# A new order of the 35 DMA transfers of a batched matmul-and-subtract kernel

## Chip, cores, metric

The kernel runs on one core of a Trainium2 chip. The metric is device time per execution in microseconds (us). A run is called slow when it is over 1.5% above the fastest of its kernel; ratios use the other runs, called fast.

## The reference

```python
batch, m, k, n = 16, 512, 1024, 768
def reference(x, weight, sub_value):          # all float32
    return (np.matmul(x, weight) - sub_value).astype(np.float32)
```

The 8192 rows are worked as 64 "m tiles" of 128. In memory terms: x is 33.6 MB, sub_value and the result 25.2 MB each, the weight 3.1 MB, 87.0 MB in all.

## The kernel before

All transfers are issued by one engine (SyncE) in the order of a table. Each entry is a kind (x, weight chunk, sub_value, output), a first tile and a number of tiles. SyncE waits for what an entry needs, issues it, and goes to the next; so a transfer whose wait isn't over also holds back those after it.

```python
TRANSFERS = [
    ('x', 0, 1), ('w', 0, 1), ('x', 1, 1), ('w', 1, 1), ('x', 2, 2), ('w', 2, 1),
    ('w', 3, 1), ('x', 4, 4), ('s', 0, 5), ('x', 8, 8), ('s', 5, 3), ('s', 8, 8),
    ...
    ('o', 48, 10), ('o', 58, 4), ('o', 62, 1), ('o', 63, 1),
]
...
            need, by = {                      # what must be done before this entry is issued
                "w": (set(), "o"),
                "x": ({t for t in old if t >= 0}, "cast"),     # the x ring holds 16 tiles
                "s": ({t for t in old if t >= 0}, "o"),        # sub_value/output ring: 32 tiles
                "o": (span, "finish"),
            }[kind]
```

ScalarE casts each x tile to fp16. The tile is then transposed, 40 tiles on TensorE (ScalarE evicts them) and 24 on VectorE. TensorE multiplies in four chunks of the weight, and VectorE subtracts sub_value in place ("finish"), after which the tile may be stored. PSUM has three output buffers, so tile 3 cannot be multiplied before tile 0 is finished. Casts, transposes and finishes run in fixed orders on their engines.

```python
NX, NSO = 16, 32
N16, NXT, NPT, NPO = 4, 5, 2, 3               # NPO: outputs in PSUM
...
    idle(9)                                   # filler matmuls that keep the TensorE clock up
    cast(2)
    cast(3)
    transpose_tile(2)
    transpose_tile(3)
    for c in range(n_c):
        matmuls(2, c)
    finish(2)
    for mi in range(HEAD + 1, HEAD + TA):     # tile 4
        cast(mi)
        transpose_tile(mi)
```

## Time and profile before

| | before |
|---|---|
| time, median of 3 runs, at the time of the prediction | 211.04 us (210.6 to 211.05) |
| span of the profiled execution | 208.5 us |
| TensorE busy | 195.9 us (94%) |
| VectorE busy | 147.4 us (71%) |
| share of the 16 DMA engines taken by the kernel's queue | 98.0% |
| bytes moved | 87.03 MB |

In the page's slice rows, each of the 40 digits is a fortieth of the span: busy tenths for an engine, tenths of full clock for PEclk, mean busy tenths of the 16 DMA engines for DMA. The thing to notice is that two resources, TensorE and DMA, look full at once, while the chain of work that ended last names only one.

### The profile page before, as it was taken

How to read it: one execution, taken by the hardware profiler on the slowest of the kernel's cores; microseconds unless marked ns; L12 is line 12 of the kernel's file. 1: busy time of each engine (PE TensorE's matmuls, PEld its weight loads, DVE VectorE, ACT ScalarE, POOL GpSimd, SP SyncE). 2: the span in 40 equal slices, each digit the busy share in tenths (PEclk: the TensorE clock that was granted, in tenths of full speed). 3: DMA queues.
4: the chain of work that ended last, by engine and by line, in shares of the span. 5: the costliest groups of instructions: out<-in, count | busy, mean ns of one | idle time of the engine just before them, and what ended most of it. 6: DMA issues, size and time to landing. Idle time of an engine off the chain costs nothing.

```text
span 208.5 us, 2449 instructions
## 1 busy us (share of the span) xinstructions
PE 195.9 (94%) x1216; PEld 75.7 (36%) x704; DVE 147.4 (71%) x266; ACT 103.1 (49%) x105; POOL 0.7 (0%) x6
## 2 busy tenths in 40 slices
PE   7959879999999999999999999999999999999970
PEld 2413434443343434343434333343434343344420
DVE  0231043369999999998899969999999999423330
ACT  2640556976446371916463275537291821467400
POOL 1000000000000000000000000000000000000000
PEclk9996999999999999999999999999999999999998
DMA  6999999999999999999999999999999999999994
GB/s 198 424 437 425 458 437 383 457 405 438 433 445 429 439 421 422 442 429 420 408 463 431 417 430 442 445 386 430 434 426 447 424 431 434 443 446 395 460 390 199
DMA packets 4906, 87.17 MB, mean 418 GB/s; under 512 B 544, under 2 KB 544, under 8 KB 1568
## 3 DMA queue, kind: packets, MB, share of 16 engines
q1 hardware_dynamic: 4896, 87.03, 98.0%
q8 instruction: 7, 0.11, 0.2%
q14 instruction: 3, 0.02, 0.0%
HBM read 61.87 MB, written 25.17 MB: 417 GB/s over the span
## 4 chain that ended last, share of the span: by engine, by line
PE 88%; DMA 5%; ACT 1%; SPq 1%; DVE 1%; issue 0%
PE po_b L180 79%; PE pt_b L317 8%; DMA so_ring<-in_weight_dram 5%; ACT xt_b L324 1%; PE po_b L405 1%; SPq L280 1%; DVE w_sb L247 0%; DVE so_ring L388 0%; ACT x_b L299 0%; SPq L244 0%; SPq L517 0%; SPq L134 0%
## 5 line engine op out<-in xcount | busy, mean ns | idle before, releaser
L180 PE MATMUL po_b<-w_sb,xt_b 128*128 128x384 f16 x640 | 113.3, 329 | 3.5 <-DVE w_sb L247 2.6
L344 DVE STREAM_TRANSPOSE xtp_b<-x16p_b 32x256 f32<-32x256 f32 x192 | 83.6, 435 | 8.2 <-ACT x16p_b L299 5.2
L388 DVE TENSOR_TENSOR so_ring<-po_b,so_ring 128x768 f32<-128x768 f32 x64 | 60.0, 956 | 34.7 <-PE po_b L180 21.6
L324 ACT COPY xt_b<-pt_b 128x1024 f16<-128x1024 f16 x40 | 40.4, 1012 | 81.4 <-PE pt_b L317 81.0
L180 PE MATMUL po_b<-w_sb,xtp_b 128*128 128x384 f16 x384 | 73.6, 326 | 0.0
L368 PEld LDWEIGHTS <-xt_b 128*128 128x128 f16 x320 | 31.7, 99 | 63.2 <-issue 60.3
L299 ACT CAST x_b<-x_ring 128x1024 f16<-128x1024 f32 x40 | 41.5, 1045 | 8.8 <-DMA x_ring<-in_x_dram 8.7
L317 PE MATMUL pt_b<-ident,x_b 128*128 128x128 f32 x160 | 41.1, 273 | 1.3 <-ACT x_b L299 1.3
L317 PEld LDWEIGHTS pt_b<-ident,x_b 128*128 128x128 f32 x160 | 22.0, 141 | 34.8 <-issue 31.6
L299 ACT CAST x16p_b<-x_ring 128x1024 f16<-128x1024 f32 x24 | 25.1, 1046 | 3.9 <-DMA x_ring<-in_x_dram 3.8
L368 PEld LDWEIGHTS <-xtp_b 128*128 128x128 f16 x192 | 18.8, 98 | 21.9 <-issue 20.1
L247 DVE CAST w_sb<-so_ring 128x768 f16<-128x768 f32 x8 | 4.1, 557 | 11.8 <-DMA so_ring<-in_weight_dram 11.8
L405 PE MATMUL po_b<-idle_x,idle_w 128*128 128x512 f16 x31 | 9.3, 454 | 1.5 <-DVE idle_x L399 1.5
L405 PEld LDWEIGHTS po_b<-idle_x,idle_w 128*128 128x128 f16 x31 | 3.5, 114 | 5.9 <-issue 2.7
L299 ACT ACT_TABLE_LOAD x1 | 1.3, 1283 | 0.9 <-SPq L134 0.9
L398 DVE MEMSET idle_w<- 128x64 uint32 x1 | 0.1, 112 | 1.0 <-SPq L134 1.0
L418 PE MATMUL po_b<-idle_x,idle_w 128*128 128x512 f16 x1 | 0.4, 379 | 0.0
L169 POOL TENSOR_SCALAR_AFFINE_SELECT ident<-ident 128x128 f32<-128x128 f32 x1 | 0.3, 292 | 0.1
L399 DVE MEMSET idle_x<- 128x256 uint32 x1 | 0.3, 272 | 0.0
L168 POOL MEMSET ident<- 128x128 f32 x1 | 0.2, 206 | 0.5 <-SPq L134 0.5
L418 PEld LDWEIGHTS po_b<-idle_x,idle_w 128*128 128x128 f16 x1 | 0.1, 98 | 0.1
L506 POOL MEMSET const-bfloat16-1.0<- 128x1 bf16 x1 | 0.1, 102 | 0.0
(3 smaller groups left out, 0.3 us busy)
## 6 DMA issues: line engine op xcount, KB each, us to landing
so_ring<-in_sub_value_dram SPq DMA_DIRECT2D x2, 3840.0 KB, 20.1
x_ring<-in_x_dram SPq DMA_DIRECT2D x2, 3584.0 KB, 18.7
x_ring<-in_x_dram SPq DMA_DIRECT2D x2, 3072.0 KB, 23.0
out_dram<-so_ring SPq DMA_DIRECT2D x2, 3072.0 KB, 30.4
out_dram<-so_ring SPq DMA_DIRECT2D x1, 6144.0 KB, 32.9
x_ring<-in_x_dram SPq DMA_DIRECT2D x1, 5120.0 KB, 17.4
so_ring<-in_sub_value_dram SPq DMA_DIRECT2D x2, 2304.0 KB, 16.7
x_ring<-in_x_dram SPq DMA_DIRECT2D x1, 4608.0 KB, 19.7
```

Of the source, the lines that this page charges most:

```text
L169: pool.add(lambda: nc.gpsimd.affine_select(out=ident, in_=ident, compare_op=mybir.AluOpType.not_equal, fill=1.0, base=0, pattern=[[-1, P]] ...
L180: return nc.tensor.add_instruction(mybir.InstMatmult(name=nc.get_next_instruction_name(), engine=full.engine, ins=list(full.ins), outs=lis ...
L247: lambda at=at, r=r, st=st: nc.vector.tensor_copy(out=w_sb[:, at, r], in_=st[:, r]),
L280: sp.add(lambda here=here, there=there: nc.sync.dma_start(out=here, in_=there), waits, (sem, 16))
L299: act.add(lambda: nc.scalar.copy(out=to, in_=x_in), waits, count("cast"))
L317: pe.add(lambda: nc.tensor.transpose(words, from_, ident), waits, count("turn") if last else None)
L324: act.add(lambda: nc.scalar.copy(out=xt_b[:, d], in_=pt_b[:, b]), waits, count("evac"))
L344: dve.add(lambda: nc.vector.transpose(xt[b * Q : (b + 1) * Q, :, a * Q : (a + 1) * Q], x16[a * Q : (a + 1) * Q, :, b * Q : (b + 1) * Q],), ...
L368: pe.add(lambda weights=weights: nc.tensor.ldweights(weights, tile_position=(0, 0)), [w for w in waits if w[0] in ready])
L388: dve.add(lambda: nc.vector.tensor_tensor(out=o, in0=po[:, :, :NS], in1=o, op=mybir.AluOpType.subtract), [landed["s", mi], (counter["mul"] ...
L405: lambda: nc.tensor.matmul(po_b[:, NPO - 1, 0], idle_w, idle_x, start=True, stop=True),
L418: pe.add(lambda: nc.tensor.matmul(po_b[:, NPO - 1, 0], idle_w, idle_x, start=True, stop=True), [(counter["ident"], 2)])
```

## The change

The intent is that each load of the steady part be asked for well before the queue has worked off what stands in front of it (at least two thirds of a transfer). The weights come ahead of x tiles 2 and 3, some transfers are cut differently, and the last store holds two m tiles instead of one.

```diff
 TRANSFERS = [
-    ('x', 0, 1), ('w', 0, 1), ('x', 1, 1), ('w', 1, 1), ('x', 2, 2), ('w', 2, 1),
-    ('w', 3, 1), ('x', 4, 4), ('s', 0, 5), ('x', 8, 8), ('s', 5, 3), ('s', 8, 8),
-    ('x', 16, 3), ('s', 16, 5), ('x', 19, 6), ('x', 25, 7), ('s', 21, 11), ('o', 0, 8),
-    ('x', 32, 7), ('o', 8, 8), ('s', 32, 6), ('x', 39, 9), ('s', 38, 10), ('x', 48, 10),
-    ('o', 16, 9), ('o', 25, 7), ('s', 48, 6), ('s', 54, 10), ('x', 58, 6), ('o', 32, 16),
-    ('o', 48, 10), ('o', 58, 4), ('o', 62, 1), ('o', 63, 1),
+    ('x', 0, 1), ('w', 0, 1), ('x', 1, 1), ('w', 1, 1), ('w', 2, 1), ('w', 3, 1),
+    ('x', 2, 2), ('x', 4, 4), ('s', 0, 4), ('x', 8, 2), ('s', 4, 4), ('x', 10, 6),
+    ('s', 8, 8), ('x', 16, 3), ('x', 19, 6), ('s', 16, 9), ('x', 25, 7), ('o', 0, 8),
+    ('s', 25, 7), ('x', 32, 6), ('o', 8, 8), ('s', 32, 5), ('x', 38, 10), ('s', 37, 11),
+    ('x', 48, 7), ('x', 55, 3), ('o', 16, 6), ('o', 22, 10), ('s', 48, 6), ('x', 58, 6),
+    ('s', 54, 10), ('o', 32, 16), ('o', 48, 10), ('o', 58, 4), ('o', 62, 2),
 ]
```

## The prediction

> **What bounds the kernel now.** I read the page's DMA and engine rows first, then engine and DMA sums over two long stretches, then the transfers' issue-to-landing times, then the start and the end in the timeline. One core, span 208.5 us in the profiled execution, 211.04 us as the median of the timed runs; I carry the difference of 2.5 us along as constant.
>
> The page, DMA part and chain:
>
> ```profile
> PEclk9996999999999999999999999999999999999998
> DMA  6999999999999999999999999999999999999994
> q1 hardware_dynamic: 4896, 87.03, 98.0%
> ...
> PE 88%; DMA 5%; ACT 1%; SPq 1%; DVE 1%; issue 0%
> ```
>
> The chain of work that ended last says "PE 88%", but it follows releases, and a transfer that stands in the DMA queue behind others is not a release. The DMA row says the other half: every slice between the first and the last is at 9 tenths or more. The sums over 3 to 103 and 103 to 203 us (columns: stretch, its length, busy us of PE, PEld, DVE, ACT, POOL with instructions, granted clock, DMA share, GB/s):
>
> ```profile
> 3.00:103.00 100.00, 95.13 (x579) 37.36 (x345) 67.22 (x122) 52.93 (x55) 0.00 (x0) 0.98 1.01 428
> 103.00:203.00 100.00, 99.21 (x636) 37.80 (x354) 79.63 (x143) 48.87 (x50) 0.00 (x0) 1.00 1.00 431
> ```
>
> The 16 DMA engines are at share 1.00 for 200 us running and move 429 GB/s. So there is no hole in the DMA stream to be filled. TensorE is also nearly always busy. The two run neck and neck, and the DMA bytes (87.03 MB) are the same before and after.
>
> How far ahead are the loads asked for already? From the DMA view cut to the moment of an issue (KB, then us to landing), the four tightest of the later part, each from its own stretch:
>
> ```profile
> x_ring<-in_x_dram SPq DMA_DIRECT2D x1, 5120.0 KB, 17.4
> ```
>
> ```profile
> so_ring<-in_sub_value_dram SPq DMA_DIRECT2D x1, 2304.0 KB, 11.9
> ```
>
> ```profile
> so_ring<-in_sub_value_dram SPq DMA_DIRECT2D x1, 3840.0 KB, 14.6
> ```
>
> ```profile
> out_dram<-so_ring SPq DMA_DIRECT2D x1, 384.0 KB, 4.0
> ```
>
> At 429 GB/s their own bytes take 12.2, 5.5, 9.2 and 0.9 us, so 5.2, 6.4, 5.4 and 3.1 us were something else. The very first transfer, with nothing before it, takes 4.1 us for 0.52 MB (1.2 us), hence 2.9 us of pure overhead. So the tightest loads stood 2.3 to 3.5 us in the queue behind others, and only the last store (0.2 us) met a queue that was about to run dry. "Ahead enough" is already true of every load.
>
> The start, from the timeline of TensorE and VectorE (start, us, engine, line, operation, count, idle before it and releaser):
>
> ```profile
> 14.45 1.03 DVE L247 CAST w_sb<-so_ring 128x768 f16<-128x768 f32 x2 [3.35 <-DMA so_ring<-in_weight_dram]
> 16.32 1.03 DVE L247 CAST w_sb<-so_ring 128x768 f16<-128x768 f32 x2 [0.85 <-DMA so_ring<-in_weight_dram]
> 25.89 2.69 DVE L388 TENSOR_TENSOR so_ring<-po_b,so_ring 128x768 f32<-128x768 f32 x3 [8.54 <-DMA so_ring<-in_sub_value_dram]
> ```
>
> ```profile
> 15.53 4.44 PE L180 MATMUL po_b<-w_sb,xt_b 128*128 128x384 f16 x16 [2.27 <-DVE w_sb L247]
> ...
> 23.45 2.77 PE L180 MATMUL po_b<-w_sb,xt_b 128*128 128x384 f16 x16 [0.67 <-ACT xt_b L324]
> 26.06 0.60 PE L317 MATMUL pt_b<-ident,x_b 128*128 128x128 f32 x4
> 26.90 0.81 PE L180 MATMUL po_b<-w_sb,xt_b 128*128 128x384 f16 x4 [0.24 <-DVE so_ring L388]
> ```
>
> TensorE waits 2.27 us for the third chunk of the weight and then runs 16 matmuls in 4.44 us instead of 2.6 because its clock fell to half. Tile 3 starts at 26.90, released by the first subtraction, which itself waited for the first sub_value load (PSUM holds three outputs, so tile 3 needs tile 0's). One more wait of 1.00 us (a cast) follows inside tile 3; after 28.7 TensorE never waits again and reaches the last matmul at 202.25.
>
> **What the Trainium skill says.** "DMA: Bandwidth & Descriptors", Specifications, gives a fabric ceiling of 435 GB/s and an HBM limit of about 358 GB/s per core. The trace sits at 429, so it agrees with the first and contradicts the second; 99% of the ceiling is reached. The same page, Anatomy of one DMA, says that DMA engines do not wait on semaphores, the issuing sequencer does, and puts about 2 us of fixed cost on a transfer (fitted on another issue path); here the first transfer shows 2.9 us. "TensorE: Matmul & The Clock Gate", Part 1, says that an idle window of about 3.4 us halves the clock. This trace halves it after 2.27 us of idleness, for one such window (the 6 in PEclk), which costs about 1.7 us of TensorE work.
>
> **The change, part by part.** No compute instruction is added or removed; 34 transfers become 35, same bytes.
>
> (a) One more transfer: 128 more packets. A 3 KB row takes 121 ns and a 48 KB row 1815 ns in the trace's packet records, so 8 ns each beyond the bytes: 128 x 8 / 16 engines = 0.06 us.
>
> (b) Weights ahead of x tiles 2 and 3. Those x tiles are 1.05 MB, 2.4 us. The third chunk lands at 14.4 - 2.4 = 12.0, its casts end at 13.0, and TensorE is done with chunk 2 at 13.3: the 2.27 us wait and the slow clock go. The fourth chunk is cast by 14.9, so chunks 3 and 4 end at about 16.2 instead of 19.97. Nine filler matmuls (1.9) follow, then transposes (0.6, x tiles 2 and 3 having landed at 16.3 and been cast at 17.3) and an eviction (1.0): tile 2 starts at about 19.9 instead of 23.45, **3.5 us earlier**, and ends at 22.6 (2.77 us), tile 4's transposes at 23.2.
>
> (c) But tile 3 waits for sub_value. Ahead of it are now 7.34 MB + a 1.57 MB load of four tiles: it lands 3.7 us (1.57 MB) after x 4 to 7, which land at 21.2 as before, so 24.9 instead of 25.85. With a subtraction of 0.96 us, tile 3 starts at **25.9 instead of 26.9**. The 3.5 us shrink to 1.0; a gap of some 2.7 us stands before tile 3, and may halve the clock there (1.7 us). The 1.00 us wait for a cast in tile 3 goes, as ScalarE gets through its queue earlier. Lead of TensorE at tile 4: 2.0 to 2.3 us, or about 0.4 with the halved clock.
>
> (d) Splitting x 8 to 15 in 2 + 6 moves x 10 to 15 from 36.3 to about 38.3-39 (14.68 MB in all). The cast of tile 12, in ScalarE's order ahead of tile 8's eviction, waits for it; tile 8's eviction ends at 40.4-41.1, just about when a TensorE that leads by 2 us wants it (41.0). VectorE's first transposes start at 42.5 instead of 43.45, and its subtraction of tile 8 then ends at 49.8 where tile 11 wants it at 49.7. So VectorE allows a lead of about 1.3 to 2 us, no more.
>
> (e) The steady part. Summing bytes at 429 GB/s and taking the releases from the casts and subtractions of the trace less 1 to 2 us, x 38 to 47 is issued at about 99 with a queue until 106, x 48 to 54 at 119 with one until 128, sub_value 48 to 53 at 146 with one until 155, 54 to 63 at 155 with one until 168. All longer than before, and worth nothing: the queue wasn't empty before. The DMA stream stays at share 1.00.
>
> (f) The last store. Before: issued at 203.25, 4.0 us. After: two tiles, 2.9 + 1.8 = 4.7 us from its issue, which comes at 203.25 less the lead. With a lead of 0.4 to 2.0 it lands on TensorE's account at 207.5 to 206.0; on the DMA queue's account at about 207.0 (207.25 less the 0.2 us of near-empty queue). The later counts: **207.0 to 207.5 against 207.25**.
>
> The sum: -0.25 to +0.25 us, plus 0.06. I put it at 210.9 us.
>
> **Rivals.** (1) *TensorE is the bound*, as the chain says: then the lead of 2 us shows in full, 209.0 us. Against it: DMA share 1.00 and bytes unchanged; 87.03 MB at 429 GB/s are 202.9 us, plus 2.2 us before the first packet and about 2 us from last byte to end, which is all of the span. (2) *The start gets worse*: gap before tile 3 with a halved clock, plus stalls on tile 12's cast and on VectorE, leave TensorE 1 us late; the two-tile store adds 0.7: 212.5 to 213 us. For it: gap and late x 10 to 15 are real. Against it: I count a lead even with the halved clock. (3) *The new mix moves faster*: slices of the GB/s row vary from 383 to 463, but that is packets counted where they start; both 100 us stretches give 428 and 431, so at most some tenths of a us.
>
> **Range and chances.** Centre 210.9; low end if the queue's tail packs better and runs fall as the fastest of before (210.6) do, 209.7; high end from rival 2, 212.8. A gain over 2% needs 206.8, below what the bytes take: 0.02. A loss over 2% needs 215.3, a TensorE late by 4 us and more: 0.04.
>
> **What would show it.** Right: DMA share 1.00 throughout; tile 2's matmuls at about 19.9; the first subtraction at about 24.9 and tile 3 at 25.9 after a gap of 2 to 3 us; ScalarE idle until 38 to 39 for x; the last subtraction ending 0.4 to 2 us before 203.2 while the span hardly moves. Wrong: a DMA slice of steady time below 9 tenths, a last subtraction later than before, or a span that follows TensorE's lead.

## The result

The changed kernel takes 210.49 us (median of 6 runs, 210.23 to 210.66), the kernel before 210.63 us in the same comparison (6 runs, 210.17 to 211.05). The ratio is 0.9991 with a 95% interval of 0.9973 to 1.0008: the same. A ratio is the mean time of one kernel's fast runs over that of the other's of the same rounds, so it is not quite the ratio of the medians quoted.

The programs of TensorE, VectorE, ScalarE and GpSimd are the same in the two kernels but for which landing they wait for; only the DMA issues differ. The page of the changed kernel, the same rows as shown of before:

```profile
PEclk9999969999999999999999999999999999999996
DMA  5999999999999999999999899999999999999984
q1 hardware_dynamic: 5040, 87.03, 98.0%
...
PE 84%; DMA 10%; SPq 2%; DVE 1%; issue 0%; DVEq 0%
```

The DMA row has the same shape and the same 98.0%. The slow slice of the clock has moved from the fourth to the sixth slice (26 to 31 us). The sums over the two long stretches (busy us and counts by engine, clock, DMA share, GB/s):

```profile
3.00:103.00 100.00, 95.97 (x583) 37.89 (x347) 68.26 (x125) 53.34 (x55) 0.00 (x0) 0.98 1.01 428
103.00:203.00 100.00, 98.56 (x632) 37.61 (x352) 78.69 (x140) 48.05 (x50) 0.00 (x0) 1.00 1.00 430
```

They show 428 and 430 GB/s, where before had 428 and 431: the stream was full and stayed full. The start, from the timeline of VectorE and TensorE:

```profile
11.79 1.03 DVE L247 CAST w_sb<-so_ring 128x768 f16<-128x768 f32 x2 [0.85 <-DMA so_ring<-in_weight_dram]
...
24.82 2.69 DVE L388 TENSOR_TENSOR so_ring<-po_b,so_ring 128x768 f32<-128x768 f32 x3 [10.11 <-DMA so_ring<-in_sub_value_dram]
```

```profile
19.71 2.78 PE L180 MATMUL po_b<-w_sb,xt_b 128*128 128x384 f16 x16 [0.67 <-ACT xt_b L324]
22.32 0.60 PE L317 MATMUL pt_b<-ident,x_b 128*128 128x128 f32 x4
...
25.83 0.81 PE L180 MATMUL po_b<-w_sb,xt_b 128*128 128x384 f16 x4 [2.91 <-DVE so_ring L388]
...
27.56 1.48 PE L180 MATMUL po_b<-w_sb,xt_b 128*128 128x384 f16 x4
```

The third weight chunk arrives 2.7 us earlier and tile 2 starts at 19.71 instead of 23.45. Then TensorE stands 2.91 us until the first subtraction, which waits for its load of sub_value; its clock halves (four matmuls take 1.48 us instead of 0.81), and of the 3.7 us lead 0.6 us are left. The last subtraction, before and after, and the store after it (KB, us to landing):

```profile
202.25 0.96 DVE L388 TENSOR_TENSOR so_ring<-po_b,so_ring 128x768 f32<-128x768 f32 x1 [1.64 <-PE po_b L180]
```

```profile
201.59 0.96 DVE L388 TENSOR_TENSOR so_ring<-po_b,so_ring 128x768 f32<-128x768 f32 x1 [1.64 <-PE po_b L180]
out_dram<-so_ring SPq DMA_DIRECT2D x1, 768.0 KB, 4.6
```

The store goes out at 202.6 and lands at 207.2. In the kernel before it was issued at 203.2 and landed at 207.25.

### The profile page after: what moved, and what is told of

Its sections match the earlier page's. It is cut to its first block, busy times and chain, and to the rows that moved or that the text cites. A ratio compares the mean times of both kernels' runs of the same rounds, so it can differ in the third digit from the quotient of the medians.

```text
span 208.5 us, 2450 instructions
## 1 busy us (share of the span) xinstructions
PE 196.1 (94%) x1216; PEld 76.1 (36%) x704; DVE 147.3 (71%) x266; ACT 102.7 (49%) x105; POOL 0.7 (0%) x6
## 4 chain that ended last, share of the span: by engine, by line
PE 84%; DMA 10%; SPq 2%; DVE 1%; issue 0%; DVEq 0%
PE po_b L180 77%; DMA so_ring<-in_sub_value_dram 10%; PE pt_b L317 7%; DVE so_ring L388 1%; SPq L244 1%; SPq L280 1%; SPq L517 0%; DVEq L56 0%; SPq L134 0%
## 5 line engine op out<-in xcount | busy, mean ns | idle before, releaser
L388 DVE TENSOR_TENSOR so_ring<-po_b,so_ring 128x768 f32<-128x768 f32 x64 | 60.0, 955 | 37.1 <-PE po_b L180 25.9
L405 PE MATMUL po_b<-idle_x,idle_w 128*128 128x512 f16 x31 | 9.9, 477 | 1.5 <-DVE idle_x L399 1.5
L418 PE MATMUL po_b<-idle_x,idle_w 128*128 128x512 f16 x1 | 0.4, 379 | 0.0
```

Of the source, the lines that this page charges most:

```text
L388: dve.add(lambda: nc.vector.tensor_tensor(out=o, in0=po[:, :, :NS], in1=o, op=mybir.AluOpType.subtract), [landed["s", mi], (counter["mul"] ...
L405: lambda: nc.tensor.matmul(po_b[:, NPO - 1, 0], idle_w, idle_x, start=True, stop=True),
L418: pe.add(lambda: nc.tensor.matmul(po_b[:, NPO - 1, 0], idle_w, idle_x, start=True, stop=True), [(counter["ident"], 2)])
```

## Experiments

Theory A: the DMA stream bounds the time, and TensorE's lead counts for nothing as long as the last store is issued before the queue is empty. Rival B: TensorE is the bound, as the chain says, and its lead was eaten by the halved clock and by the longer last store. "Lead" means how much earlier a matmul starts than the same matmul in the one profile of the kernel before. Two profiles of one order already differ by up to 0.3 us in this count, as e2 shows below, so a lead is good to about that.

### Four edits of the ends: e1 to e4

e1 is the changed kernel with two single stores at the end:

```diff
-    ... ('o', 62, 2),
+    ... ('o', 62, 1), ('o', 63, 1),
```

> The changed order, with the last two m tiles stored by two transfers again. Theory A (the DMA stream is the bound; TensorE's lead counts only in the last microsecond): the dip of the DMA share at 202 to 204 us goes, the last landing moves from 207.2 to 206.8-207.0, the time is 0.2 to 0.5 us below the changed kernel, so about 0.3 us below the kernel before (ratio 0.998). Rival B (TensorE is the bound and its lead of 0.66 us is what counts): the whole 0.66 us shows, and a lone one-tile store saves another 0.6: about 1.2 us below the kernel before (0.994).

e2 is the kernel before with the opposite edit, its last two stores made one.

> The kernel before with only its last two stores made one. Both theories: TensorE ends at 202.2 as before, the store is issued at 203.2 and takes 4.6-4.7 us instead of 4.0, so 0.5 to 0.7 us slower than the kernel before (ratio 1.002 to 1.003). A rival C, that one larger store is cheaper at the end because it has one completion less: 0.1 to 0.3 us faster.

e3 is the changed kernel with fillers in the gap before tile 3 (into a transposition buffer whose content has been evicted). e4 is e3 with e1's stores.

```diff
     for mi in range(HEAD + 1, HEAD + TA):
         cast(mi)
         transpose_tile(mi)
+    for _ in range(13):
+        pe.add(
+            lambda: nc.tensor.matmul(pt_b[:, 1].bitcast(F32), idle_w, idle_x, start=True, stop=True),
+            [(counter["evac"], evac_at[3])],
+        )
```

> The changed kernel with 13 filler matmuls in the gap before tile 3, so that the clock is not halved. Both theories: no half-speed window at 26 to 31 us, TensorE's lead over the kernel before grows from 0.66 to about 2 us, the last subtraction starts near 200.2. Theory A: the span falls by at most 0.3 us against the changed kernel (last landing 206.9), because the DMA queue ends when it ends. Rival B: the span falls by the whole 1.3 us, to 207.2 (ratio to the kernel before 0.993).

> Fillers in the gap and two single stores at the end: the best that the parts promise. Theory A: no more than e1 or e3 alone, last landing 206.7 to 206.9, ratio to the kernel before 0.997 to 0.999. Rival B: lead 2 us and a short last store, 2.5 us less, ratio 0.988.

All four are correct, and ran on one chip with the same runs of the kernel before (median 210.94, 11 runs between 210.32 and 212.31, a noisier set than elsewhere):

| run | median us | ratio to before (95%) | lead at tile 4 | lead at tile 62 |
|---|---|---|---|---|
| changed kernel (earlier comparison) | 210.49 | 0.9991 (0.9973 to 1.0008) | 0.61 | 0.65 |
| e1 split last store | 210.62 | 0.9975 (0.9943 to 1.0007) | 2.13 | 0.80 |
| e2 merged last store, old order | 210.56 | 0.9982 (0.9945 to 1.0019) | 0.29 | -0.20 |
| e3 fillers in the gap | 210.72 | 0.9983 (0.995 to 1.0016) | 2.35 | 0.73 |
| e4 both | 210.45 | 0.997 (0.9938 to 1.0002) | 2.20 | 0.66 |

None differs from the kernel before beyond its interval, and the ratios that Rival B gave for e3 (0.993) and e4 (0.988) lie outside the intervals measured. e2 issues the same transfers as the kernel before up to its last store and has the same compute, so its 0.29 and -0.20 are what chance alone does to a lead. The clock row and a timeline line of e3:

```profile
PEclk9999999999999999999999999999999999999997
```

```profile
22.68 2.97 PE L446 MATMUL pt_b<-idle_x,idle_w 128*128 128x512 f16 x13
25.76 0.81 PE L180 MATMUL po_b<-w_sb,xt_b 128*128 128x384 f16 x4
```

The fillers do what they should: no halved clock, and a lead of 2.35 us at tile 4. The time does not follow, which Rival B needed. The second thing in the table wasn't expected in this form: all leads of the new order end at 0.65 to 0.80 us. In e3 the lead is 2.35 at tile 6, 1.36 at tile 12 and 0.71 at tile 40. The first cut comes where the prediction put it, at tiles 8 to 12, where TensorE waits for VectorE's subtractions (matmuls released by it at 50 and 53 us). The second comes at tiles 38 to 40, again released by VectorE; VectorE's transposes of tile 40 wait there 2.23 us for a cast, and the cast 2.71 us for the load of x 38 to 47, which lands at 119.5. So the DMA stream itself takes the lead back.

By chance e1's profiled run shows the same without fillers:

```profile
25.98 0.81 PE L180 MATMUL po_b<-w_sb,xt_b 128*128 128x384 f16 x4 [2.92 <-DVE so_ring L388]
```

Its gap before tile 3 was 2.92 us long, yet its clock did not halve. The clock records say what the chance was. While the kernel runs, the granted clock changes only at steps of 3.41 us, whose position differs from run to run. Here is the step before the halved one and the halved one, in the kernel before and in the changed one, and the two steps over which e1's gap lies (PE's busy time comes third; the clock is the third number from the end):

```profile
12.22:15.63 3.41, 1.14 (x8) 0.29 (x3) 1.03 (x2) 1.99 (x2) 0.00 (x0) 1.00 1.06 438
15.63:19.05 3.42, 3.42 (x12) 0.87 (x6) 1.03 (x2) 0.00 (x0) 0.00 (x0) 0.50 1.00 426
```

```profile
23.71:27.12 3.41, 1.29 (x9) 0.47 (x5) 2.30 (x3) 2.15 (x3) 0.00 (x0) 1.00 1.04 428
27.12:30.53 3.41, 3.41 (x13) 1.32 (x8) 0.39 (x1) 0.00 (x0) 0.00 (x0) 0.50 1.06 449
```

```profile
20.87:24.28 3.41, 2.20 (x15) 0.96 (x9) 0.00 (x0) 2.22 (x3) 0.00 (x0) 1.00 0.97 407
24.28:27.70 3.42, 1.72 (x12) 0.71 (x7) 2.69 (x3) 1.73 (x2) 0.00 (x0) 1.00 1.03 426
```

TensorE was busy for 33% and 38% of the steps that a halved one follows; e1's gap was split, and left 64% and 50%. Counted over all 14 traces, the 35 full-clock steps that a halved one follows are busy for at most 0.44 of their length, the 752 that a full one follows for at least 0.40. (Busy times of matmuls are modelled, so the border is rough.)

The clock also gives a test without new runs. Of e1's six runs, three have a mean clock of 0.992, the profiled one among them, and took 210.35, 210.67 and 210.75 us; the three with a halved step (0.977 to 0.982) took 210.47, 210.58 and 210.79. TensorE's gain does not show in the time.

e2 lost nothing, against an expected 0.5 to 0.7 us. Its end and that of the changed kernel, by microsecond (the last two columns are DMA share and GB/s):

```profile
202.00:203.00 1.00, 0.41 (x3) 0.00 (x0) 0.56 (x1) 0.00 (x0) 0.00 (x0) 1.00 0.92 393
203.00:204.00 1.00, 0.00 (x0) 0.00 (x0) 0.40 (x1) 0.00 (x0) 0.00 (x0) 1.00 0.55 233
204.00:205.00 1.00, 0.00 (x0) 0.00 (x0) 0.00 (x0) 0.00 (x0) 0.00 (x0) 1.00 0.89 375
```

```profile
202.00:203.00 1.00, 0.00 (x0) 0.00 (x0) 0.55 (x1) 0.00 (x0) 0.00 (x0) 1.00 0.92 393
203.00:204.00 1.00, 0.00 (x0) 0.00 (x0) 0.00 (x0) 0.00 (x0) 0.00 (x0) 1.00 0.87 369
204.00:205.00 1.00, 0.00 (x0) 0.00 (x0) 0.00 (x0) 0.00 (x0) 0.00 (x0) 0.81 0.93 387
```

The queue does run thin in e2 (0.55 at 203 to 204 us), but its store, issued at 203.4, lands 4.0 us later at 207.4, only 0.15 us after the one-tile store of before. So this dip costs a few tenths at most, and these are not seen in the times.

### Relieving one bound, then the other: e5 to e7

Three kernels with wrong results, all from the changed kernel. e5 leaves out half of the matmuls, e6 stores only the first half of the tiles of each store, e7 does both.

```diff
     def matmuls(mi, c):                       # e5, e7
+        if c in (1, 2):
+            return
...
             if kind == "o":                   # e6, e7
-                here, there = there, here
+                keep = max(1, n // 2)
+                here, there = there[:, :keep], here[:, :keep]
```

> The changed kernel with the matmuls of chunks 2 and 3 of the four left out (a wrong result on purpose): TensorE has about 94 us less to do, all transfers as before. Theory A: the DMA share stays at 1.00 and the time falls by at most 0.6 us, 209.7 to 210.5. Rival B (TensorE bounds): tens of microseconds less, 120 to 160 us.

> The changed kernel with each store halved to its first half of the tiles (a wrong result on purpose): 12.6 MB less, 29 us of the DMA stream. Theory A with TensorE close behind: TensorE's own chain (start at 25.8, 175.8 us of work to 201.6, subtraction, store) takes over as the bound, so the time falls by little, 1 us at most (the last store is one tile and not two): 209.5 to 210.3. A pure DMA bound with TensorE far behind would give 181 us.

> Both reliefs at once (wrong on purpose). Theory A (two bounds neck and neck): only now does the time fall much, to about 178 to 188 us, the DMA stream of 74.4 MB at 429 GB/s (173.5 us) plus start and end and what VectorE's and ScalarE's chains hold back. If neither alone nor both moved it, a third bound (VectorE, 147 us busy, or ScalarE) would be the one.

| run | TensorE busy us | MB | median us | ratio to before (95%) |
|---|---|---|---|---|
| e5 half of the matmuls | 131.0 | 87.0 | 210.33 | 0.9995 (0.998 to 1.0009) |
| e6 half of the stores | 195.7 | 74.5 | 207.37 | 0.9859 (0.9842 to 0.9875) |
| e7 both | 126.9 | 74.5 | 193.47 | 0.9194 (0.918 to 0.9207) |

e5, its engine row and DMA row, and the last store (KB, us to landing), issued at 192.1:

```profile
PE 131.0 (63%) x704; PEld 51.8 (25%) x448; DVE 147.2 (71%) x266; ACT 102.2 (49%) x105; POOL 0.7 (0%) x6
...
DMA  6999999999999999999999999999999999999993
```

```profile
out_dram<-so_ring SPq DMA_DIRECT2D x1, 768.0 KB, 15.2
```

This is the clearest result. A third of TensorE's busy time is gone (65 us, not the 94 that I had expected), the last store is ready more than 10 us earlier, and it lands at 207.3 all the same, after 15.2 us mostly in the queue. The DMA stream sets the end, and the chain view, which had said "PE 88%", had not seen it. That view is no steady witness either: in e1, which computes the same, it says

```profile
DMA 40%; PE 36%; DVE 10%; ACT 6%; SPq 2%; issue 2%; ACTq 0%
```

e6 shows how close the second bound is. Its DMA row and last store:

```profile
DMA  5999999999999999999799999999999995009031
```

```profile
out_dram<-so_ring SPq DMA_DIRECT2D x1, 384.0 KB, 2.3
```

Here the queue is empty at the end, TensorE's chain ends as in the changed kernel (last subtraction at 201.6), and the time is 3.0 us lower. I had expected 1 us at most, because I had taken 2.9 us of overhead for a transfer that meets an empty queue. The measured store takes 2.3 us for 0.39 MB; less 0.9 us for its bytes at 429 GB/s, that is 1.4. e6's two longer stores before it, and all three such stores of e7, give 1.4 to 1.5 as well. So TensorE's chain would end 1.4 us before the DMA stream in the changed kernel, not with it: the two profiled spans, both with a halved clock at the start, differ by 2.3 us (208.5 and 206.2), less the 0.9 us by which e6's one-tile store is shorter. The median of e6 is lower by more because three of its four runs kept the full clock (0.998 to 1.0) and took 207.25 to 207.47 us, against 207.97 for the profiled one (0.986). Here, where TensorE is the bound, the halved step costs 0.5 to 0.7 us; in e1 it cost nothing.

e7 lands above its expected 178 to 188. The chain of e7:

```profile
DVE 65%; DMA 17%; PE 7%; issue 5%; SPq 3%; ACT 2%; ACTq 0%
```

With both relieved, the chain names VectorE's transposes and subtractions. But the chain was wrong above, and from 62 to 172 us two resources are full again, VectorE with 106.98 us of 110 and DMA with a share of 0.99:

```profile
62.00:172.00 110.00, 71.70 (x406) 27.47 (x242) 106.98 (x203) 56.35 (x58) 0.00 (x0) 0.94 0.99 416
```

No run relieves VectorE, so which of them sets e7's time is not shown. What is shown: relieving DMA alone is worth 1.4%, relieving TensorE and DMA together 8%.

### The start alone: e8

The kernel before with only the weights moved ahead of x tiles 2 and 3.

```diff
-    ('x', 0, 1), ('w', 0, 1), ('x', 1, 1), ('w', 1, 1), ('x', 2, 2), ('w', 2, 1),
-    ('w', 3, 1), ('x', 4, 4), ...
+    ('x', 0, 1), ('w', 0, 1), ('x', 1, 1), ('w', 1, 1), ('w', 2, 1), ('w', 3, 1),
+    ('x', 2, 2), ('x', 4, 4), ...
```

> The kernel before with only the weights moved ahead of x tiles 2 and 3, all other transfers as before. Both theories: tile 2's matmuls start near 19.8, the first subtraction at 25.9 as before, tile 3 at 26.9 after a gap of 3.7 us with a halved clock after it; the wait of 1.0 us for a cast in tile 3 goes. TensorE's lead between -0.7 and +1.0 us. Theory A: time within 0.5 us of the kernel before unless TensorE comes out late; rival B: it follows the lead one to one.

Measured: 210.28 us, ratio 0.9996 (0.9981 to 1.0011). TensorE gains 3.8 us at tile 2, and loses all of it in one wait:

```profile
26.70 0.99 PE L180 MATMUL po_b<-w_sb,xt_b 128*128 128x384 f16 x4 [3.84 <-DVE so_ring L388]
27.49 0.42 PE L317 MATMUL pt_b<-ident,x_b 128*128 128x128 f32 x1
27.70 1.49 PE L180 MATMUL po_b<-w_sb,xt_b 128*128 128x384 f16 x4
```

The clock halves, and TensorE runs 0.26 us behind the kernel before from then on and 0.21 behind at the end, no more than e2 does at the end (0.20). The time is the same, as theory A has it. The weights' early place gives TensorE a lead past tile 3 only together with the shorter first load of sub_value.

### What the longer lead is worth: e9 to e12

If loads that are asked for early are worth nothing in an undisturbed run, they should be worth something when a load is late. In e9 (old order) and e10 (new order) every load of x from tile 32 on waits for two more m tiles of TensorE; in e11 and e12 only the load of x from tile 48 on does.

```diff
             if kind == "x" and need:
                 waits.append((counter["cast"], max(cast_at[t] for t in need)))
+                if at >= 32:                  # e9, e10;  in e11, e12: if at == 48
+                    waits.append((counter["mul"], so_far["mul"] + 2))
```

> The kernel before with every load of x from tile 32 on held back until TensorE has done two more m tiles. Theory A: the load of x 48 to 57 is issued 4.1 us later (128.3 instead of 124.2), which is 1.1 us more than the queue held (5.1 us to the landing before it[...]), so a hole of about 1.1 us opens in the DMA stream near 129 and the time rises by 0.8 to 1.3 us. If loads needed no lead: no change.

> The changed kernel with the same hold-back of x loads. Theory A: its loads stood 7.8 us and more before the landing ahead of them, so delays of 3.2 to 5.8 us open a hole of 0.1 us at most, and the time stays within 0.3 us of the changed kernel: here, and only here, the longer lead of the new order is worth something (about 1 us against the same hold-back in the old order).

e9 took 215.38 us (six runs from 213.78 to 217.52), ratio 1.0214 (1.0169 to 1.0259); its profiled run is the slow one of them, so I read no size from it. e10 took 213.12 us, 1.0136 (1.0109 to 1.0163). Both expectations were too low, e10's by a factor of ten. In e10 the load of x 38 is issued at 105.1, which leaves 2.0 us to the landing ahead of it, and the DMA share falls to 0.36 in 105 to 106 us:

```profile
105.00:106.00 1.00, 1.00 (x9) 0.29 (x3) 0.97 (x2) 0.74 (x1) 0.00 (x0) 1.00 0.36 138
```

This is a load for which the new order asks later, not earlier, relative to the queue: in the undisturbed profiles x 38 is issued 7.8 us before the landing ahead of it, and its counterpart in the old order, x 39, 8.8 us. The load at tile 48 went the other way, from 5.1 to 7.9. This trial also feeds back on itself: loads wait for TensorE, which waits for loads. So I ran it with one load:

> The kernel before with one load alone, x from tile 48 on (its tightest), held back by two more m tiles of TensorE. In the first hold-back trial (all x loads from 32 on) this load left a hole of 1.4 us in the DMA stream, its first packets then took 2.1 us instead of 1.5, and TensorE starved later. Theory A, as it now stands: the hole returns (1.2 to 1.5 us), restart 0.6 us, so 1.5 to 3 us slower (ratio 1.007 to 1.014), less than the 4.8 us of that trial because no later load repeats the delay. If the hole alone cost: 1.0 to 1.4 us.

> The changed kernel with the same hold-back of its load of x from tile 48 on. Issue moves from 121.4 to about 124.6, the landing ahead of it is at 129.3, so 4.7 us remain[...]: no hole, time within 0.4 us of the changed kernel (ratio to the kernel before 0.997 to 1.002). If the earlier trial's 2.9 us came from this load and not from the load of x 38: about 2 us slower.

e11 took 213.96 us (213.88 to 215.23), ratio 1.0172 (1.0148 to 1.0195). e12 took 210.50 us (one of six runs at 212.63, the others 210.32 to 210.63), ratio 1.0012 (0.9978 to 1.0046). The same hold-back of one load costs the old order 3.6 us (1.72% of 210.6) and the new order nothing that shows. It moved the issue by 3.9 us in e11 and by 3.2 in e12, and left 1.2 and 4.9 us to the landing ahead. The load was chosen as the old order's tightest; e10 shows that the new order isn't safe everywhere. e11, then e12, around the late load (DMA share and GB/s last):

```profile
127.00:128.00 1.00, 1.00 (x9) 0.55 (x5) 0.97 (x3) 0.00 (x0) 0.00 (x0) 1.00 0.37 139
128.00:129.00 1.00, 1.00 (x8) 0.32 (x4) 0.97 (x3) 0.71 (x1) 0.00 (x0) 1.00 0.00 0
129.00:130.00 1.00, 1.00 (x9) 0.29 (x3) 0.97 (x3) 1.00 (x2) 0.00 (x0) 1.00 2.15 655
130.00:131.00 1.00, 1.00 (x7) 0.29 (x3) 0.97 (x2) 1.00 (x2) 0.00 (x0) 1.00 0.00 0
```

```profile
127.00:128.00 1.00, 1.00 (x9) 0.43 (x4) 0.97 (x3) 0.14 (x1) 0.00 (x0) 1.00 1.16 479
128.00:129.00 1.00, 1.00 (x8) 0.29 (x3) 0.96 (x4) 1.00 (x2) 0.00 (x0) 1.00 0.93 401
```

A packet counts where it starts, so "2.15 655" and "0.00 0" in turn say that after the hole all 16 engines start their packets within half a microsecond of each other; in e12 they stay staggered. The packet records put the hole at 1.5 us of idle engines. The first packets after it take 2.15 us where 1.51 is usual, and the last ones of that transfer 2.72 where before has 1.57. Together 1.5 + 0.6 + 1.2 = 3.3 us, most of the 3.8 us by which the load lands later (145.4 instead of 141.6). Every later landing is then late by about as much: the last one is at 211.2 instead of 207.25. Why packets that start together are slower, no run tells. How early is early enough can be estimated from three fast runs: the time that was left to the landing ahead and the idle time of the engines that followed add up to 2.7 us in e10 (1.95 + 0.77), 2.8 in e11 (1.23 + 1.53) and 3.0 in e6 (1.15 + 1.87, its load of x 38). So a load should be issued some 3 us before the landing ahead of it.

No experiment gave a version that beats both kernels: e4, the best of the parts, has an interval that includes 1.

## Why the prediction was right or wrong

- **DMA is the bound, TensorE close behind: right, and shown** by e5 (TensorE relieved, no change) against e6 (DMA relieved, 3.0 us). A detail of the sum against rival 1 is off: 202.9 + 2.2 + 2 us reach the last landing at 207.25, not all of the span, which goes on to 208.5.
- **The start (b and c): right.** Tile 2 at 19.71 (predicted 19.9), first subtraction at 24.82 (24.9), tile 3 at 25.83 (25.9) after a gap of 2.91 us (some 2.7), clock halved, lead 0.61 us (about 0.4 with the halved clock; within the 0.3 us that leads scatter).
- **VectorE's cap on the lead (d): the mechanism was right, the size too generous.** The x load landed at 39.3 and VectorE's first transposes began at 43.2, not 42.5. Without a halved clock the lead after tile 12 is 1.34 us in e1, 1.37 in e3 and 0.92 in e4 (1.3 to 2 was predicted), and a second cut at tile 40, which the prediction did not have, leaves 0.6 to 0.8.
- **The steady part (e): right in what it says of the time.** Loads are issued as listed (99.4, 121.4, 147.3 and 156.3 against 99, 119, 146 and 155), the stream stays at 1.00, and the time does not move. "All longer than before" is wrong for x 38 (7.8 us to the landing ahead, where x 39 had 8.8). That the longer lead is "worth nothing" holds only for an undisturbed run: e11 and e12 show what it insures.
- **The fixed cost in the last store (f): wrong in size.** The prediction took 2.9 us from the first transfer of the kernel, which is a load. Stores that meet an empty queue have 1.4 us (e6, e7). So the last store of before stood 1.7 us in the queue (4.0 - 0.9 - 1.4), not 0.2; the two-tile store took the predicted 4.6 to 4.7 us, but 1.4 of them were queue (4.6 - 1.8 - 1.4), and it landed on the DMA queue's account at 207.2, within the predicted 207.0 to 207.5. That its length came out right is luck, two errors that cancel. TensorE and DMA were not as neck and neck as the prediction said: TensorE has 1.4 us to spare.
- **The number:** 210.9 predicted, 210.49 measured, inside the range; the predicted gain or loss against before was -0.25 to +0.25 us plus 0.06, the medians differ by 0.14. Most of the miss is the starting point: the kernel before came out at 210.63 with more runs, not 211.04, and the constant 2.5 us between span and time set the span of one execution against the median of others (that execution was timed at 210.34, 1.8 us above its span).

## What to carry to other kernels

Here the DMA share was 1.00 from end to end, and none of the orders tried made the kernel faster, whatever the chain of releases said; test such a case by relieving the engine that the chain names. The lead that TensorE gained at the start was taken back by the next fixed order and the next landing that it met. Count how long before the landing ahead of it each load is issued: beyond some 3 us more of it gained no time here, but it is what keeps a late load from opening a hole, and in e11 a hole cost more than twice its width.

## What the Trainium skill lacked or had wrong

- "DMA: Bandwidth & Descriptors", Specifications: the row with the HBM limit of about 358 GB/s for a core is half of a stack's 716 and no bound for a core that streams alone, as the page's section on bandwidth itself says (in its part on where 436 GB/s comes from, the sentence that the HBM side binds between HBM and SBUF needs the same condition). The prediction used the row without that condition. The runs, on one core, hold 428 to 431 GB/s for 200 us, close to the fabric ceiling of 435.
- The same page, Anatomy of one DMA: about 2 us of fixed cost, fitted on another issue path. A 384 KB store into an empty queue took 2.3 us in e6, and it and five longer ones in e6 and e7 took 1.4 to 1.5 us beyond their bytes; the kernel's first load took 2.9 us beyond its bytes. One number for both directions is too coarse here.
- The same page says nothing that I found of what a dry queue costs when it fills again: 1.5 us of idle engines made the load land 3.8 us later (e11), with first packets of 2.15 us instead of 1.51.
- "TensorE: Matmul & The Clock Gate", Part 1: an idle window of about 3.4 us halves the clock. Here gaps of 2.27 and 2.91 us, shorter than that, halved it, for 3.4 us. A gap of 2.92 us in e1 did not, which agrees with what the page says of a free-running window. The page gives no figure for how busy such a window may be: those that led to a halved clock here were busy for up to 0.44 of their length.
